# Decoder trunk: rows of x loaded ahead of the modulation weights, and the first channel tile's modulation multiplied by one-column matmuls

## The chip, the core and the metric

One core of a Trainium2 chip runs the whole kernel. TensorE (PE, with its weight loads shown apart as PEld), VectorE (DVE), ScalarE (ACT), GpSimd (POOL) and SyncE (SP) work in parallel, each through its own list of instructions in order. DMAs are issued from the queues of SP, ACT and POOL. Operands lie in SBUF; matmul results lie in PSUM. The metric is the device time of one execution in microseconds (us), lower is better.

## What is computed

A decoder layer over 512 tokens of 1024 channels. What the change touches is its first step, the modulated normalisation and the projection behind it:

```python
cs = jax.nn.silu(c)
...
mod = cs @ w_ada[l] + b_ada[l]
shift1, scale1, gate1, shift2, scale2, gate2 = [m[:, None, :] for m in jnp.split(mod, 6, axis=-1)]
h = _rmsnorm(x, norm1_g[l]) * (1.0 + scale1) + shift1
proj = h @ w_in[l]
```

`_rmsnorm` divides each row of x by the root of its mean square (plus 1e-6) and multiplies by the gain. Behind it stand two attention branches, a gated merge, an output projection and a gated MLP with a short convolution; they are the same before and after.

## The kernel before

The 512 tokens are four row tiles of 128 (`NT`), the 1024 channels eight channel tiles of 128 (`KT`). A large product in float32 is made of three: each operand is split into a rounded high part (type fp32r, a copy) and a low part (the difference), and high x high, low x high and high x low are added in PSUM.

**The first stage** (lines 198 to 413) makes h, transposed to channels x tokens, and the first 768 columns of the projection (six banks `acc6`, one of 128 columns each). It goes by channel tile k. For each, two column blocks of `w_ada` are needed (scale and shift, 8 x 128 rows x 128 columns each, tile `adaw`, two buffers) and one row block of `w_in` (`w0`, 128 x 768, four buffers).

- **Loads** stand on SP's queue in written order (lines 154 and 211 to 226): the conditioning vector c, `adaw` of tile 0, the four row tiles of x (512 KB each), `w0` of tile 0, then `adaw` and `w0` of tile 1, and so on. Bias and gain rows come on ACT's queue (lines 157 to 159).
- **Modulation** of tile k: `ac_ops` multiplies each of the eight row blocks of `adaw` by its entry of silu(c), one value per partition, and sums them, on DVE, 256 columns at a time; `reduce_mod` sums over the partitions by two matmuls with a column of ones; `finish_mod` adds bias and gain, giving one scale and one shift per channel (`mods`).
- **Statistics** of row tile t: `stat` squares on ACT (with the sum) and takes the power -1/2 on POOL (line 174) between DVE steps (lines 170, 180, 184); `normalise` multiplies the first 256 channels on DVE (line 352), `scale_x` the other 768 on ACT (line 375). `turn` transposes channel tile 0 of one row tile on PE (line 357), `h_turn` the later channel tiles.
- **h of tile k**: `h_tile` writes the high part and a full copy on ACT, with scale and shift (line 317); `h_low` makes the low part on DVE (line 321).
- **Weights**: `split_hi` makes the high part of `w0` on ACT (lines 296 and 297, with a reordering of the first 512 columns), `split_lo` the low part on DVE (lines 303 and 305).
- **Products**: `mm_k` runs 6 matmuls for each of three parts (line 327). While tile k multiplies, DVE makes the modulation of tile k + 1.
- `keep_warm(n)` issues n matmuls of ones whose result is not used (line 335), each shown as two PE instructions; 14 stand at the start and 3 behind each row tile.

The order on DVE, ACT and PE is the written one in this stage (`manual_schedule`). In it, before the loop, DVE has the copy of the bias columns `cols`, the modulation of tile 0, and then per row tile t the statistics of t ahead of the normalising of t - 1; the low parts of `w0` of tile 0 come last, directly ahead of the modulation of tile 1 in the loop.

SP's and POOL's queues are ordered by the framework; `va`, a zeroed tile of the attention stage (line 435), is set on POOL early, before the first power.

Of the kernel before, what the change touches and what calls it, by code (L numbers as in the profile page):

```python
# [14 lines left out]
P = 128  # L15
# [11 lines left out]
WB = 3  # L27
# [7 lines left out]
NORM_LAG = 16  # L35
SWA_FILL = (4, 2, 3, 2, 2, 2, 2, 3)
DIFF_FILL = (3, 2, 4, 2)
WARM = 14
GROUPS = ((0,), (1,), (2,), (3,), (4,), (5,), (6,), (7,))
AC_CUT = 7  # L40
MOD_AT = 2
# [11 lines left out]
def kernel(  # L53
# [44 lines left out]
    def tbank(name, shape=(P, S)):  # L98
        return bank("t", 2, list(shape), name)
# [4 lines left out]
    def raw_tile(shape, name):  # L104
        return wp.tile(shape, F32, tag="raw", bufs=4, name=name)
# [45 lines left out]


    crow8 = cpool.tile([8, P], F32, name="crow8")
    nc.sync.dma_start(crow8, c.rearrange("o (a p) -> (o a) p", p=P))
    NR = 16 + 8 + 1
    rows = cpool.tile([NR, P], F32, name="rows")
    nc.scalar.dma_start(rows[0:16, :], b_ada[0, 0 : 2 * D].rearrange("(a p) -> a p", p=P))
# [9 lines left out]
    def rstd_start(ssq, n, d, wpool, plus=None):  # L167
        ms = wpool.tile([P, n], F32, tag="rs_a", bufs=3, name="ms")
        if plus is None:
            nc.vector.tensor_scalar(ms, ssq, 1.0 / d, EPS, ALU.mult, ALU.add)  # L170
        else:
            nc.vector.scalar_tensor_tensor(ms, ssq, 1.0 / d, plus, ALU.mult, ALU.add)  # L172
        r0 = wpool.tile([P, n], F32, tag="rs_c", bufs=3, name="r0")
        nc.gpsimd.tensor_tensor(r0, ms, mhalf[:, :n], ALU.pow)  # L174
        return ms, r0
# [23 lines left out]
    groups = GROUPS  # L199
    adaw, w0 = {}, {}  # L200

    def load_ada(g):
        k, m = g[0], len(g)
        aw = pp.tile([P, 2, KT, m * P], F32, tag="adaw", bufs=2, name=f"adaw{k}")
        for j, base in ((0, D), (1, 0)):
            nc.sync.dma_start(
                aw[:, j], wada[:, base + k * P : base + (k + m) * P].rearrange("(a p) n -> p a n", p=P)
            )
        adaw[k] = aw

    load_ada(groups[0])
    for t in range(NT):
        nc.sync.dma_start(xn[:, t], xd[t * P : (t + 1) * P, :])
    for g in groups:
        if g[0]:
            load_ada(g)
        for k in g:
            r = raw_tile([P, 768], f"w0_{k}")
            nc.sync.dma_start(r, win[k * P : (k + 1) * P, 0:768])
            w0[k] = r  # L220
    nc.sync.dma_start(sink, swa_sinks[0].partition_broadcast(P))
    nc.sync.dma_start(
        lamv.rearrange("p a b -> p (a b)"), diff_lambda[0].rearrange("a b -> (a b)").partition_broadcast(P)
# [8 lines left out]
    nc.vector.tensor_scalar_add(cs, cs, 1.0)  # L232
    nc.vector.reciprocal(cs, cs)
    nc.vector.tensor_mul(cs, cs, pc8)
    pc = tbank("pc", (P, NR))
    nc.tensor.transpose(pc, rows, ident[:NR, :NR])
    cols = cpool.tile([P, NR], F32, name="cols")
    nc.vector.tensor_copy(cols, pc)
    bsh, bsc1, n1g, sublnc = cols[:, 0:8], cols[:, 8:16], cols[:, 16:24], cols[:, 24:25]
    nc.vector.tensor_scalar_add(bsc1, bsc1, 1.0)  # L240
    nc.vector.tensor_scalar_mul(n1g, n1g, -0.5)
    nc.vector.tensor_scalar_mul(sublnc, sublnc, -0.5 * (1.0 - LAM_INIT))
    ac, mods, wts = {}, {}, {}

    def ac_ops(gi, lo, hi):
        g = groups[gi]
        if lo == 0:
            ac[gi] = [pp.tile([P, 2, len(g) * P], F32, tag=f"ac{b}", bufs=2, name=f"ac{gi}_{b}") for b in range(2)]
        aw = adaw[g[0]]
        for kk in range(lo, hi):  # L250
            a = ac[gi][kk % 2]
            if kk < 2:
                nc.vector.tensor_scalar_mul(a, aw[:, :, kk], cs[:, kk : kk + 1])
            else:
                nc.vector.scalar_tensor_tensor(a, aw[:, :, kk], cs[:, kk : kk + 1], a, ALU.mult, ALU.add)
        if hi == KT:
            nc.vector.tensor_add(ac[gi][0], ac[gi][0], ac[gi][1])

    def reduce_mod(gi):
        pas = []  # L260
        for i, k in enumerate(groups[gi]):
            pa = tbank(f"pa{k}", (P, 2))
            for j in range(2):
                nc.tensor.matmul(
                    pa[:, j : j + 1], ac[gi][0][:, j, i * P : (i + 1) * P], ones[:, 0:1], start=True, stop=True
                )
            pas.append(pa)
        return pas

    def finish_mod(gi, pas):  # L270
        for k, pa in zip(groups[gi], pas):
            m = pp.tile([P, 16], F32, tag="mod", bufs=3, name=f"mod{k}")
            nc.vector.scalar_tensor_tensor(
                m[:, 0:1], pa[:, 0:1], bsc1[:, k : k + 1], n1g[:, k : k + 1], ALU.add, ALU.mult
            )
            nc.vector.tensor_add(m[:, 1:2], pa[:, 1:2], bsh[:, k : k + 1])
            mods[k] = m
# [12 lines left out]
    def split_hi(k):  # L290
        pl, nb = (wp, WB) if k % 2 == 0 else (pp, 2)
        wh = pl.tile([P, 768], F32R, tag="whi", bufs=nb, name=f"w0h{k}")
        wl = pl.tile([P, 768], F32R, tag="wlo", bufs=nb, name=f"w0l{k}")
        wts[k] = (wh, wl)
        rq, wq, lq = w0_views(k)
        nc.scalar.copy(wq, rq)
        nc.scalar.copy(wh[:, 512:768], w0[k][:, 512:768])

    def split_lo(k, part):
        wh, wl = wts[k]  # L300
        if part == 0:
            rq, wq, lq = w0_views(k)
            nc.vector.tensor_tensor(lq, rq, wq.bitcast(F32), ALU.subtract)
        else:
            nc.vector.tensor_sub(wl[:, 512:768], w0[k][:, 512:768], wh[:, 512:768].bitcast(F32))
# [8 lines left out]
    def h_tile(k):  # L314
        hf = pp.tile([P, S], F32, tag="hf", bufs=2, name=f"hf{k}")
        for dst in (hTh[k], hf):
            nc.scalar.activation(dst, pts[k], AF.Identity, bias=mods[k][:, 1:2], scale=mods[k][:, 0:1])
        hfs[k] = hf
# [4 lines left out]
    def mm_k(k, part):  # L323
        wh, wl = wts[k]
        lhs, rhs = ((wh, hTh), (wl, hTh), (wh, hTl))[part]
        for i in range(6):
            nc.tensor.matmul(
                acc6[i], lhs[:, i * P : (i + 1) * P], rhs[k],
                start=k == 0 and part == 0, stop=k == KT - 1 and part == 2,
            )  # L330


    def keep_warm(n):
        for i in range(n):
            nc.tensor.matmul(acc6[5][:, :P], ident, ones, start=True, stop=True)

    keep_warm(WARM)
    ac_ops(0, 0, KT)
    rst = pp.tile([P, NT], F32, name="rst")
    half = [None] * NT  # L340

    def stat(t):
        sq = pp.tile([P, D], F32, tag="sq", bufs=1, name=f"sq{t}")
        ss = pp.tile([P, 1], F32, tag="ss", bufs=4, name=f"ss{t}")
        nc.scalar.activation(sq, xn[:, t], AF.Square, accum_out=ss)
        half[t] = rstd_start(ss, 1, D, pp)

    HEAD = 256

    def normalise(t):  # L350
        rstd_end(rst[:, t : t + 1], *half[t], 1, pp)
        nc.vector.tensor_scalar_mul(xn[:, t, :HEAD], xn[:, t, :HEAD], rst[:, t : t + 1])

    pts[0] = tbank("xt0")

    def turn(t):
        nc.tensor.transpose(pts[0][:, t * P : (t + 1) * P], xn[:, t, 0:P], ident)

    for t in range(NT):
        stat(t)  # L360
        if t:
            normalise(t - 1)
            turn(t - 1)
            keep_warm(3)
        if t == 1:
            finish_mod(0, reduce_mod(0))
    split_hi(0)
    normalise(NT - 1)
    turn(NT - 1)
    h_tile(0)  # L370
    split_lo(0, 0)
    split_lo(0, 1)

    def scale_x(t):
        nc.scalar.activation(xn[:, t, HEAD:], xn[:, t, HEAD:], AF.Copy, scale=rst[:, t : t + 1])

    for gi, g in enumerate(groups):
        nxt = groups[gi + 1] if gi + 1 < len(groups) else ()

        for k in nxt:  # L380
            split_hi(k)
        if gi == 0:
            for t in range(NT):
                scale_x(t)

        if nxt:
            ac_ops(gi + 1, 0, AC_CUT)
        h_low(g[0])
        if nxt:
            ac_ops(gi + 1, AC_CUT, KT)  # L390

        for k in g:
            if k == g[0] and len(nxt) == 1:
                h_turn(nxt[0])
            for part in range(3):
                if part == MOD_AT and k == g[-1] and nxt:
                    pas = reduce_mod(gi + 1)
                    split_lo(nxt[0], 0)
                    finish_mod(gi + 1, pas)
                    split_lo(nxt[0], 1)  # L400
                    for n in nxt[1:]:
                        split_lo(n, 0)
                        split_lo(n, 1)
                    for n in nxt:
                        if len(nxt) > 1:
                            h_turn(n)
                        h_tile(n)
                mm_k(k, part)
            if k == g[0]:
                for n in g[1:]:  # L410
                    h_low(n)
# [1313 lines left out]
```

## Time and profile before

| | us |
|---|---|
| median of 3 runs | 722.17 (719.83 to 722.52) |
| the profiled execution | 720.56 |
| its span in the trace | 718.7 |
| first product matmul of tile 0 starts | 18.47 |
| first instruction of tile 1's modulation on DVE | 16.74 |
| last product matmuls of the first stage end | about 59.9 |

Over the span PE is busy 691.1 us (96%), DVE 589.8 (82%), ACT 381.9 (53%) and POOL 84.9 (12%); DMA reads 121.85 MB. A timeline row gives the start, the duration, the engine, the line, the operation with its output and inputs, how many were merged, and in brackets the idle time of the engine before it with what ended it. A merged row's duration runs from the first start to the last end. The stretches table gives the busy time of each engine within a stretch of time, the granted PE clock (1.00 is full) and what the DMA engines moved.

### The profile page before, as it was taken

The numbers are of one execution on the slowest core, as the hardware profiler recorded it, in microseconds if no ns is written. First come the engines' busy times: TensorE is split into PE (matmuls) and PEld (weight loads), VectorE is DVE, ScalarE is ACT, GpSimd is POOL, SyncE is SP. The second block draws the span as 40 slices with busy tenths as digits, with TensorE's granted clock in tenths as the row PEclk, the third lists the DMA queues.
The fourth block names the chain that finished last, engine by engine and source line by source line (L and its number), as shares of the span: only waits on it lengthen the run. The fifth ranks groups of instructions, "written<-read, shape, count | busy, mean of one in ns | idle before, by whom it ended". The sixth has DMA issues, their size and how long they took to land. (4 is left out here: it accounts for less than half of the span.)

```text
span 718.7 us, 11251 instructions
## 1 busy us (share of the span) xinstructions
PE 691.1 (96%) x4172; PEld 603.1 (84%) x4172; DVE 589.8 (82%) x1121; ACT 381.9 (53%) x672; POOL 84.9 (12%) x101
## 2 busy tenths in 40 slices
PE   6998899999999999999999999999999999999994
PEld 6776688777777888888888999999999999778883
DVE  6998877887986674865479899888888999889996
ACT  4643756355553333432358756555656666556662
POOL 4000000000100110000012111111101212640000
PEclk9999999999999999999999999999999999999998
DMA  9986122543543665736717698876879769998502
GB/s 313 305 242 205 60 60 67 169 136 106 169 139 126 206 190 162 235 101 210 246 59 148 162 190 204 207 183 200 201 197 223 161 175 256 206 207 221 178 0 118
DMA packets 117367, 124.70 MB, mean 174 GB/s; under 512 B 4511, under 2 KB 93376, under 8 KB 117312
## 3 DMA queue, kind: packets, MB, share of 16 engines
q1 hardware_dynamic: 98254, 97.71, 43.0%
q0 software_dynamic: 18720, 25.73, 21.0%
q8 instruction: 33, 0.54, 0.3%
q10 hardware_dynamic: 338, 0.54, 0.2%
q14 instruction: 22, 0.18, 0.1%
HBM read 121.85 MB, written 2.11 MB: 172 GB/s over the span
## 5 line engine op out<-in xcount | busy, mean ns | idle before, releaser
L1112 PE MATMUL up<-t,m_whi 128*128 128x256 f32 x528 | 96.1, 283 | 0.0
L1112 PEld LDWEIGHTS up<-t,m_whi 128*128 128x128 f32 x528 | 82.4, 192 | 0.0
L1112 PE MATMUL up<-t,m_wlo 128*128 128x256 f32 x264 | 74.7, 283 | 0.1
L1112 PE MATMUL up<-bh,p_wlo 128*128 128x256 f32 x232 | 65.6, 283 | 0.3 <-DVE p_wlo L1055 0.3
L1112 PE MATMUL up<-bh,p_whi 128*128 128x256 f32 x232 | 65.6, 283 | 0.0
L1112 PE MATMUL up<-bl,p_whi 128*128 128x256 f32 x232 | 65.6, 283 | 0.0
L1112 PEld LDWEIGHTS up<-t,m_wlo 128*128 128x128 f32 x264 | 50.6, 192 | 0.3 <-DVE m_wlo L1055 0.3
L748 DVE SCALAR_TENSOR_TENSOR arow<-ra,cs,arow 128x512 f32<-128x512 f32 x56 | 41.9, 748 | 4.3 <-DMA ra<-in_w_ada_dram 3.6
L1112 PEld LDWEIGHTS up<-bh,p_wlo 128*128 128x128 f32 x232 | 44.5, 192 | 0.5 <-DVE p_wlo L1055 0.5
L1112 PEld LDWEIGHTS up<-bh,p_whi 128*128 128x128 f32 x232 | 44.5, 192 | 0.0
L1112 PEld LDWEIGHTS up<-bl,p_whi 128*128 128x128 f32 x232 | 44.5, 192 | 0.0
L1023 POOL DMA_DIRECT2D s<-in_w_up_dram x21 | 27.3, 1379 | 142.5 <-DMA s<-in_w_up_dram 54.3
L1055 DVE TENSOR_TENSOR m_wlo<-s,m_whi 128x1024 fp32r<-128x1024 f32 x31 | 37.7, 1217 | 2.0 <-ACT m_whi L1051 2.0
L1051 ACT CAST m_whi<-s 128x1024 fp32r<-128x1024 f32 x31 | 32.5, 1047 | 8.5 <-PE up L1112 4.6
L174 POOL TENSOR_TENSOR r<-ms,mhalf 128x1 f32<-128x1 f32 (+1 forms) x16 | 13.6, 848 | 172.4 <-DVE ms L172 105.7
L1112 PE MATMUL up<-t,p_whi 128*128 128x256 f32 x176 | 32.2, 283 | 0.0
L678 ACT ACTIVATE sd<-sd,dmx 128x128 f32<-128x128 f32 (+3 forms) x32 | 17.8, 557 | 22.2 <-DVE dmx L676 15.7
L761 POOL DMA_DIRECT2D mod_rows<-arow x8 | 4.3, 541 | 203.5 <-ACT arow L760 203.4
L1112 PEld LDWEIGHTS up<-t,p_whi 128*128 128x128 f32 x176 | 27.5, 192 | 0.0
L1119 ACT ACTIVATE gT<-a,cv 128x512 f32<-128x512 f32 x22 | 17.7, 814 | 17.6 <-DVE a L1154 17.3
L1051 ACT CAST p_whi<-wa 128x1024 fp32r<-128x1024 f32 x18 | 18.8, 1043 | 12.0 <-PE up L1112 7.2
L1112 PE MATMUL up<-t,p_wlo 128*128 128x256 f32 x88 | 24.9, 283 | 0.0
(476 smaller groups left out, 2120.8 us busy)
## 6 DMA issues: line engine op xcount, KB each, us to landing
ra<-in_w_ada_dram SPq DMA_DIRECT2D x32, 512.0 KB, 4.2
wa<-in_w_up_dram SPq DMA_DIRECT2D x22, 512.0 KB, 4.2
s<-in_w_up_dram SPq DMA_DIRECT2D x21, 512.0 KB, 4.8
s<-in_w_up_dram POOLq DMA_DIRECT2D x21, 512.0 KB, 6.7
adaw<-in_w_ada_dram SPq DMA_DIRECT2D x16, 512.0 KB, 5.0
w<-in_w_in_dram SPq DMA_DIRECT2D x12, 512.0 KB, 4.8
a<-in_w_up_dram SPq DMA_DIRECT2D x11, 512.0 KB, 4.7
b<-in_w_down_dram SPq DMA_DIRECT2D x10, 512.0 KB, 3.6
```

The lines of the kernel that those rows point to most:

```text
L174: nc.gpsimd.tensor_tensor(r0, ms, mhalf[:, :n], ALU.pow)
L678: nc.scalar.activation(pm[m], pm[m], AF.Exp, bias=mx[:, m : m + 1], scale=slope, accum_out=lsum[:, m : m + 1])
L748: nc.vector.scalar_tensor_tensor(ac, r[:, a], cc, ac, ALU.mult, ALU.add)
L761: nc.gpsimd.dma_start(mod_rows[idx : idx + 1, hf * S : (hf + 1) * S], row)
L1023: nc.gpsimd.dma_start(dst, upblock(*blk), accum_op=ALU.add)
L1051: nc.scalar.copy(W[J, name][0], R[J, SRC[name]])
L1055: nc.vector.tensor_sub(lo, R[J, SRC[name]], hi.bitcast(F32))
L1112: nc.tensor.matmul(o[u], w[:, k, cu], b[:, k], start=name in ("p1", "m5", "p2") and k == 0 and x == 0, stop=k == 3 and x == 2, skip_group_ ...
L1119: nc.scalar.activation(grow(j), av[J][:, u], AF.Identity, bias=cv[:, 66 + j : 67 + j], scale=cv[:, 44 + j : 45 + j])
```

## The change

It touches the first stage only.

- c is loaded on ACT's queue. On SP's queue, x rows 0 to 2 come first, then the scale half of tile 0's `adaw` in two pieces, x row 3 in two halves, the shift half in three pieces, `w0` of tile 0 in two pieces, and the rest as before, with tile 1's `adaw` in four pieces.
- Tile 0's modulation leaves DVE. `first_mod` multiplies each 128 x 128 block of `adaw` by the matching column of silu(c) on PE, 16 matmuls with one moving column, summed in PSUM. Scale and shift columns are then finished on DVE as before.
- The written order becomes: statistics, normalising and turn of row tile 0, the columns `cols`, then row tiles 1 to 3 likewise, with the pieces of `first_mod` and two of the four `scale_x` between them. Row tile 3 is squared in two halves. The initial `keep_warm` is 8 in place of 14, and the later ones are two of 2 in place of three of 3.
- For tile 0, the high part of the first 512 columns of `w0` is made on DVE in place of ACT, and the high and low parts come after the modulation is finished. `mm_k(0, ...)` takes its six column groups in the order 4, 5, 0, 1, 2, 3.

```diff
-WARM = 14
+WARM = 8
...
-    nc.sync.dma_start(crow8, c.rearrange("o (a p) -> (o a) p", p=P))
+    nc.scalar.dma_start(crow8, c.rearrange("o (a p) -> (o a) p", p=P))
...
-    load_ada(groups[0])
-    for t in range(NT):
-        nc.sync.dma_start(xn[:, t], xd[t * P : (t + 1) * P, :])
...
+    adaw[0] = pp.tile([P, 2, KT, P], F32, tag="adaw", bufs=2, name="adaw0")
+    for t in range(NT - 1):
+        load_x(t)
+    load_first(0, (0, 4, 8))
+    load_x(NT - 1, (0, S, D))
+    load_first(1, (0, 4, 6, 8))
+    load_w0(0, (512, 768))
+    load_w0(0, (0, 512))
+    for g in groups[1:]:
+        load_ada(g, (0, 4, 8) if g[0] == 1 else (0, 8))
+        load_w0(g[0])
...
-        for i in range(6):
+        for i in (4, 5, 0, 1, 2, 3) if k == 0 else range(6):
...
-    keep_warm(WARM)
-    ac_ops(0, 0, KT)
...
+        for lo, hi in ((0, D),) if t < NT - 1 else ((0, S), (S, D)):
+            sq = pp.tile([P, D], F32, tag="sq", bufs=1, name=f"sq{t}_{lo}")
+            ss = pp.tile([P, 1], F32, tag="ss", bufs=5, name=f"ss{t}_{lo}")
+            nc.scalar.activation(sq[:, lo:hi], xn[:, t, lo:hi], AF.Square, accum_out=ss)
+            if hi < D:
+                nc.vector.tensor_scalar(ss, ss, 1.0 / D, EPS, ALU.mult, ALU.add)
+                plus = ss
+        half[t] = rstd_start(ss, 1, D, pp, plus)
...
+    keep_warm(WARM)
+    stat(0)
+    normalise(0)
...
+    turn(0)
+    keep_warm(2)
+    pc = tbank("pc", (P, NR))
+    nc.tensor.transpose(pc, rows, ident[:NR, :NR])
+    cols = cpool.tile([P, NR], F32, name="cols")
+    nc.vector.tensor_copy(cols, pc)
...
+    pa0 = tbank("pa0", (P, 2))
+    stat(1)
+    normalise(1)
+    turn(1)
+    keep_warm(2)
+    stat(2)
+
+    def first_mod(j, lo, hi):
+        for kk in range(lo, hi):
+            nc.tensor.matmul(
+                pa0[:, j : j + 1], adaw[0][:, j, kk], cs[:, kk : kk + 1], start=kk == 0, stop=kk == KT - 1
+            )
+
+    first_mod(0, 0, 4)
+    scale_x(0)
+    normalise(2)
+    first_mod(0, 4, 8)
+    turn(2)
+    stat(3)
+    scale_x(1)
+    first_mod(1, 0, 4)
+    m0 = mods[0] = pp.tile([P, 16], F32, tag="mod", bufs=3, name="mod0")
+    nc.vector.scalar_tensor_tensor(m0[:, 0:1], pa0[:, 0:1], bsc1[:, 0:1], n1g[:, 0:1], ALU.add, ALU.mult)
+    normalise(3)
+    first_mod(1, 4, 6)
+    turn(3)
+    first_mod(1, 6, 8)
+    nc.vector.tensor_add(m0[:, 1:2], pa0[:, 1:2], bsh[:, 0:1])
...
+    nc.scalar.copy(wts[0][0][:, 512:768], w0[0][:, 512:768])
+    rq, wq, lq = w0_views(0)
+    nc.vector.tensor_copy(wq, rq)
+    split_lo(0, 1)
     h_tile(0)
+    scale_x(2)
+    scale_x(3)
     split_lo(0, 0)
-    split_lo(0, 1)
```

More of the change, by code (lines that the diff above doesn't have):

```diff
@@ L200, with load_ada, load_x, load_first @@
     adaw, w0 = {}, {}
-    def load_ada(g):
+    def load_ada(g, cuts=(0, KT), whole=()):
         k, m = g[0], len(g)
[L204 to L209, printed above, removed]
-    load_ada(groups[0])
-    for t in range(NT):
-        nc.sync.dma_start(xn[:, t], xd[t * P : (t + 1) * P, :])
[L214 to L220, printed above, removed]
+        aw = adaw[k] = pp.tile([P, 2, KT, m * P], F32, tag="adaw", bufs=2, name=f"adaw{k}")
+        for lo, hi in zip(cuts, cuts[1:]):
+            for j, base in ((0, D), (1, 0)):
+                src = wada[lo * P : hi * P, base + k * P : base + (k + m) * P].rearrange("(a p) n -> p a n", p=P)
+                nc.sync.dma_start(aw[:, j, lo:hi], src)
+    def load_x(t, cols=(0, D)):
+        for lo, hi in zip(cols, cols[1:]):
+            nc.sync.dma_start(xn[:, t, lo:hi], xd[t * P : (t + 1) * P, lo:hi])
+    def load_first(j, cuts):
+        base = (D, 0)[j]
+        for lo, hi in zip(cuts, cuts[1:]):
+            src = wada[lo * P : hi * P, base : base + P].rearrange("(a p) n -> p a n", p=P)
+            nc.sync.dma_start(adaw[0][:, j, lo:hi], src)
+    def load_w0(k, cuts=(0, 768)):
+        if k not in w0:
+            w0[k] = raw_tile([P, 768], f"w0_{k}")
+        for lo, hi in zip(cuts, cuts[1:]):
+            nc.sync.dma_start(w0[k][:, lo:hi], win[k * P : (k + 1) * P, lo:hi])
+    adaw[0] = pp.tile([P, 2, KT, P], F32, tag="adaw", bufs=2, name="adaw0")
[9 more added lines that the diff above has]
+        load_w0(g[0])
     nc.sync.dma_start(sink, swa_sinks[0].partition_broadcast(P))
@@ L234 @@
     nc.vector.tensor_mul(cs, cs, pc8)
[L235 to L242, printed above, removed]
     ac, mods, wts = {}, {}, {}
@@ L342, in stat, with scale_x @@
     def stat(t):
[L343 to L346, printed above, removed]
+        plus = None
+        for lo, hi in ((0, D),) if t < NT - 1 else ((0, S), (S, D)):
[6 more added lines that the diff above has]
+        half[t] = rstd_start(ss, 1, D, pp, plus)
     HEAD = 256
+    def scale_x(t):
+        nc.scalar.activation(xn[:, t, HEAD:], xn[:, t, HEAD:], AF.Copy, scale=rst[:, t : t + 1])
     def normalise(t):
@@ L357, in turn @@
         nc.tensor.transpose(pts[0][:, t * P : (t + 1) * P], xn[:, t, 0:P], ident)
[L359 to L369, printed above, removed]
+    turn(0)
[4 more added lines that the diff above has]
+    nc.vector.tensor_copy(cols, pc)
+    bsh, bsc1, n1g, sublnc = cols[:, 0:8], cols[:, 8:16], cols[:, 16:24], cols[:, 24:25]
+    nc.vector.tensor_scalar_add(bsc1, bsc1, 1.0)
+    nc.vector.tensor_scalar_mul(n1g, n1g, -0.5)
+    nc.vector.tensor_scalar_mul(sublnc, sublnc, -0.5 * (1.0 - LAM_INIT))
+    pa0 = tbank("pa0", (P, 2))
[24 more added lines that the diff above has]
+    nc.vector.tensor_add(m0[:, 1:2], pa0[:, 1:2], bsh[:, 0:1])
+    wts[0] = tuple(wp.tile([P, 768], F32R, tag=f"w{b}", bufs=WB, name=f"w0{b}0") for b in ("hi", "lo"))
+    nc.scalar.copy(wts[0][0][:, 512:768], w0[0][:, 512:768])
+    rq, wq, lq = w0_views(0)
+    nc.vector.tensor_copy(wq, rq)
+    split_lo(0, 1)
     h_tile(0)
+    scale_x(2)
+    scale_x(3)
     split_lo(0, 0)
-    split_lo(0, 1)
-    def scale_x(t):
-        nc.scalar.activation(xn[:, t, HEAD:], xn[:, t, HEAD:], AF.Copy, scale=rst[:, t : t + 1])
     for gi, g in enumerate(groups):
@@ L381 @@
             split_hi(k)
-        if gi == 0:
-            for t in range(NT):
-                scale_x(t)
         if nxt:
```

## The prediction

> **What bounds the kernel now.** I read the busy table by stretches of time first, then the timeline of the first 40 us, then the clock column in half-microsecond stretches. The loop over the eight channel tiles runs until about 60 us:
>
> ```profile
> 30.00:35.00 5.00, 4.90 (x26) 3.88 (x25) 4.81 (x15) 1.92 (x5) 0.00 (x0) 1.00 0.88 264
> ```
>
> The columns are PE, PEld, DVE, ACT, POOL, clock, DMA share and GB/s. DVE is busy 4.81 of 5.00 us and PE 4.90, ACT 1.92, and DMA moves 264 GB/s. Which of DVE and PE sets the pace shows in the first instruction of each tile's modulation on DVE:
>
> ```profile
> 16.74 0.61 DVE L253 TENSOR_SCALAR ac<-adaw,cs 128x256 f32<-128x256 f32 x2
> ...
> 22.42 0.61 DVE L253 TENSOR_SCALAR ac<-adaw,cs 128x256 f32<-128x256 f32 x2
> ...
> 27.90 0.61 DVE L253 TENSOR_SCALAR ac<-adaw,cs 128x256 f32<-128x256 f32 x2
> ...
> 33.24 0.61 DVE L253 TENSOR_SCALAR ac<-adaw,cs 128x256 f32<-128x256 f32 x2
> ...
> 37.40 0.52 PEld L264 LDWEIGHTS pa<-ones,ac 128*128 128x128 f32 x4 [0.46 <-issue]
> ...
> 38.58 0.61 DVE L253 TENSOR_SCALAR ac<-adaw,cs 128x256 f32<-128x256 f32 x2
> ```
>
> The period settles at 38.58 - 33.24 = 5.34 us, and PE stands 0.46 us ahead of its reduction, which I read as the wait for the DVE sum that it reduces. So DVE paces this stage, and what counts is **when DVE begins tile 1's modulation, 16.74 now**. The first two periods (5.68 and 5.48) hold 0.48 us of DVE waiting beyond 5.34. After the loop, work follows from work, and I find nothing tied to absolute time; a shift goes to the end one for one.
>
> **What precedes 16.74.**
>
> ```profile
> 1.19 1.03 SPq L206 DMA_DIRECT2D adaw<-in_w_ada_dram  x2
> ...
> 4.72 1.80 POOL L435 MEMSET va<- 128x2048 f32 x1
> ...
> 7.11 2.46 DVE L255 SCALAR_TENSOR_TENSOR ac<-adaw,cs,ac 128x256 f32<-128x256 f32 x6
> 8.32 1.06 ACT L345 ACTIVATE sq<-xn 128x1024 f32<-128x1024 f32 x1 [5.35 <-DMA xn<-in_x_dram]
> 9.29 0.19 ACT L345 ACTIVATION_READ_ACCUMULATOR sq<-xn 128x1 f32 x1
> ...
> 11.29 0.35 DVE L352 TENSOR_SCALAR xn<-xn,rst 128x256 f32<-128x256 f32 x1
> 11.70 0.14 PEld L357 LDWEIGHTS xt<-ident,xn 128*128 128x128 f32 x1 [0.68 <-DVE xn L352]
> ...
> 11.87 0.83 PE L335 MATMUL a<-ones,ident 128*128 128x128 f32 x6
> ...
> 12.54 0.50 PE L264 MATMUL pa<-ones,ac 128*128 128x1 f32 x4
> 13.08 0.22 DVE L273 SCALAR_TENSOR_TENSOR mod<-pa,cols 128x1 f32<-128x1 f32 x1 [1.44 <-PE pa L264]
> ...
> 13.22 0.15 DVE L276 TENSOR_TENSOR mod<-pa,cols 128x1 f32<-128x1 f32 x1
> ```
>
> Tile 0's modulation, which the change takes off DVE, was under way at 7.11, while the first x rows landed only at 8.32: DVE had nothing else to do then. DVE keeps the written order: the 1.44 us before 13.08 is DVE standing for a PE result that was queued behind a transpose and warming matmuls. That kind of wait decides the new order.
>
> **The change, part by part.**
>
> *Loads.* From the first adaw issue to x0's landing is 8.32 - 1.19 = 7.13 us, for 1.05 MB of adaw and 0.52 MB of x.
>
> ```profile
> 3.50:4.00 0.50, 0.00 (x0) 0.00 (x0) 0.38 (x3) 0.00 (x0) 0.50 (x2) 1.00 1.13 342
> ...
> 7.50:8.00 0.50, 0.50 (x5) 0.50 (x4) 0.50 (x3) 0.00 (x0) 0.00 (x0) 1.00 1.00 401
> ```
>
> At 342 and 401 GB/s that is 3.07 + 1.31 us of moving and 2.75 us of delay. With the conditioning vector on ACT's queue, x0 can be issued at about 0.74, where SP starts now (an estimate: 1.19 less one issue), and lands at 0.74 + 2.75 + 1.31 = 4.8; x1 at 6.1, x2 7.4, the scale half 9.0, x3 10.3, the shift half 11.8, w0 12.8, tile 1's weights 15.8. The gain at the source is real: 3.5 us for x0.
>
> *The row chain.* The squares of x0 end at 4.8 + 1.16 = 6.0, but the power runs on POOL, whose memset of va ends at 6.52 (same place in POOL's queue, as nothing ahead of it changes). From there on the pace is that of one tile's statistics:
>
> ```profile
> 13.79 0.35 DVE L352 TENSOR_SCALAR xn<-xn,rst 128x256 f32<-128x256 f32 x1
> 14.06 0.15 DVE L170 TENSOR_SCALAR ms<-ss 128x1 f32<-128x1 f32 x1
> ...
> 14.35 0.70 POOL L174 TENSOR_TENSOR r<-ms,mhalf 128x1 f32<-128x1 f32 x1 [0.18 <-DVE ms L170]
> ...
> 15.08 0.22 DVE L180 SCALAR_TENSOR_TENSOR rt<-r,ms 128x1 f32<-128x1 f32 x1
> 15.34 0.16 DVE L184 SCALAR_TENSOR_TENSOR rst<-rt,r 128x1 f32<-128x1 f32 x1
> ...
> 15.53 0.35 DVE L352 TENSOR_SCALAR xn<-xn,rst 128x256 f32<-128x256 f32 x1
> ```
>
> From ms to xn is 15.53 - 14.06 = 1.47 us, and the next ms follows xn by 14.06 - 13.79 = 0.27. Before, ms of tile t+1 was written ahead of the normalising of tile t, so that POOL's time was covered; now the order is stat, normalise, stat, normalise, and each tile pays 1.74. Tile 0: power 6.55, xn 7.73 to 8.08, transpose 8.14.
>
> *The columns.* DVE's next instruction is the copy of cols, which waits for a PE transpose placed behind the turn and two warming matmuls (four instructions).
>
> ```profile
> 4.86 0.27 PE L236 MATMUL pc<-ident,rows 25*128 25x25 f32 x1 [2.10 <-DMA rows<-in_diff_subln_g_dram]
> 5.05 6.16 PE L335 MATMUL a<-ones,ident 128*128 128x128 f32 x28
> 5.16 0.19 DVE L238 COPY cols<-pc 128x25 f32<-128x25 f32 x1 [1.21 <-PE pc L236]
> 5.38 1.17 DVE L240 TENSOR_SCALAR cols<-cols 128x8 f32<-128x8 f32 x1
> 5.46 1.10 DVE L241 TENSOR_SCALAR cols<-cols 128x8 f32<-128x8 f32 x1
> ...
> 14.20 0.41 PE L357 MATMUL xt<-ident,xn 128*128 128x128 f32 x1 [1.15 <-DVE ms L170]
> ...
> 14.40 1.50 PE L335 MATMUL a<-ones,ident 128*128 128x128 f32 x6
> ...
> 15.69 0.42 PE L357 MATMUL xt<-ident,xn 128*128 128x128 f32 x1
> ```
>
> Seven PE instructions took 15.69 - 14.20, 0.213 us each, at the low clock; six took 12.54 - 11.87, 0.112 each, at the high one. The 28 at the start fit the low one (27 x 0.213 + 0.42 = 6.17), so PE starts cold although the clock column, which has no entry yet, prints 1.00. Hence pc at 8.14 + 5 x 0.213 = 9.21, the copy at 9.51, and four short issues (0.22 and 0.08 each) later ms1 at 9.97. Squares of x1 have been ready since 7.3, so this wait is new and costs some 2.2 us of the head start. Then xn1 11.44 to 11.79, turn 11.85; xn2 13.18; ms3 (with its extra half-row step) 13.6, power 13.9 to 14.6.
>
> *Modulation on PE.* Sixteen one-column matmuls are 32 PE instructions, since two are x4 in the row at 12.54: 0.125 us each there. The trace has none at the low clock; the bounds are 0.125 and 0.213, and I take 0.213, because loading 128x128 weights is the bulk of both kinds. The clock:
>
> ```profile
> 14.00:14.50 0.50, 0.30 (x2) 0.30 (x3) 0.46 (x4) 0.09 (x1) 0.32 (x2) 0.81 1.15 348
> ...
> 17.50:18.00 0.50, 0.50 (x5) 0.42 (x3) 0.50 (x2) 0.36 (x1) 0.00 (x0) 0.78 1.15 344
> ```
>
> It falls to half at 14.31 (0.38 of the first stretch at half) and returns at 17.72, 3.5 us after PE became steadily busy at 14.20; at the start it took about 6 us, from 4.86 to the end of the 28. In the new order PE has holes until the turn at 11.85, so release comes between 15.4 and 17.9; I take 17.7. The Trainium skill, "TensorE: Matmul & The Clock Gate", Part 1, says that the gate judges activity in free-running windows of about 3.4 us; the spacing 17.72 - 14.31 = 3.41 agrees, and by that rule alone release could come at any point from 15.3 to 18.7, that is +2.7 to +4.1 instead of one value.
>
> PE from 11.85: turn and four warming instructions to 12.92; scale half, 16 x 0.213, to 16.33. DVE's m0 scale stands ahead of normalise(3): 16.37, then xn3 16.96 to 17.31, 2.4 us later than the power allowed. PE: turn(2) to 16.54, twelve of the shift half (5.5 slow, 6.5 fast) to 18.52, turn(3) 18.65, the last four 19.15. m0 shift at 19.19. DVE then does the copy that ACT did, and both low parts.
>
> ```profile
> 15.80 0.68 DVE L303 TENSOR_TENSOR w0l<-w,w0h 128x512 fp32r<-128x512 f32 x1
> ...
> 16.40 0.42 DVE L305 TENSOR_TENSOR w0l<-w,w0h 128x256 fp32r<-128x256 f32 x1
> ```
>
> They issue 0.60 and 0.34 apart; the 512-wide copy I price as the 512-wide subtraction, 0.60 (from 0.35, the 256-wide xn, to 0.68). 19.33 + 0.60 + 0.34 + 0.60 = 20.87 for tile 1's modulation: 4.13 late. The 0.48 us of early DVE waits goes away, as PE is done by then. **Sum: +3.65 us.** At 0.125 throughout, m0 shift comes at 16.70, DVE at 18.38: +1.16. At 0.213 throughout, 20.20 and 21.88: +4.66. Scaling x on ACT and the six channel groups' order cost nothing: ACT is idle 3 us of each 5.
>
> **Rivals.** (1) *Not slower: data sets the pace.* If DVE met no wait (power overlapped, columns and modulation done in PE's holes), xn3 would follow x3: landing 10.3, half-row square 0.8, chain 1.8, DVE 12.9, tile 1 at 14.5, its weights landing in halves from 14.3. That is 2.2 + 0.48 = 2.7 us faster. For it: the loads do arrive so. Against: the 1.44 us wait shows that order binds; it decides from where m0 shift is ready before 13. (2) *Matmuls of one column count as idle* and PE stays cold into tile 0's product: +4.66, and twelve product matmuls at twice their 3.2 us end 1.4 us after the DVE sum: up to +6. (3) *PE releases early or short ones aren't slowed:* +1.2 to +2.6. (4) *Tile 2's weights come late:* their slot is now freed by PE at 19.15, not by DVE at 9.57, and SP's later loads queue behind.
>
> ```profile
> DMA to landing us min/median/max: 3.7/5.0/9.5
> ```
>
> With 0.5 us for the second issue they land at 24.7, against 20.87 + 5.34 = 26.2; at 9.5 us it is +3 more, +6.6 in all. (5) *The shift is absorbed later:* 0.
>
> **How the numbers follow.** The profiled execution took 720.56 us (span 718.7); the three runs' median is 722.17. The mean of the four is 721.3, and I add to it: 725.0, own range 723.9 (release at 15.4) to 726.0 (no release by then). Chances: forecast 0.45; (2) and (4) together 0.18, at 726 to 728; (3) 0.17, at 722.5 to 723.9; (5) 0.05, 721.3; (1) 0.15, 718.6. The range 721 to 728 leaves out (1) and little else. About 0.5% (3.6 us) is what can be told from no change: three quarters of the forecast, with the spread of the runs, and all of (2) and (4) are slower, 0.52; of (1) half reaches faster, 0.08; the rest is 0.40.
>
> **What would show it.** Right: DVE idle before the cols copy and before both m0 steps with PE as releaser, ms instructions 1.7 us apart, half clock while the one-column matmuls run, tile 1's first DVE instruction near 21, periods of 5.34 behind it. Wrong: that instruction before 17, or DMA as the releaser of xn and m0, or a pitch of 0.125 at the low clock.

## The result, and the profile after

| | before | after |
|---|---|---|
| median of 5 runs, us | 721.78 (719.83 to 722.52) | 725.76 (724.65 to 726.66) |
| ratio to before, 95% interval | | 1.0059 (1.0044 to 1.0074) |
| the profiled execution, us | 720.56 | 725.57 |
| tile 1's modulation begins on DVE, us | 16.74 | 21.64 |
| ACT takes up the first stage's last bank, us | 58.82 | 63.50 |

The kernel became 0.6% slower, 3.98 us by the medians; the forecast was 725.0. The timeline of DVE in the kernel after, from the copy of the columns to tile 3's modulation:

```profile
9.52 0.18 DVE L382 COPY cols<-pc 128x25 f32<-128x25 f32 x1 [1.66 <-PE pc L380]
...
9.96 0.14 DVE L170 TENSOR_SCALAR ms<-ss 128x1 f32<-128x1 f32 x1
...
11.49 0.15 DVE L170 TENSOR_SCALAR ms<-ss 128x1 f32<-128x1 f32 x1
...
18.01 0.22 DVE L409 SCALAR_TENSOR_TENSOR mod<-pa,cols 128x1 f32<-128x1 f32 x1 [4.58 <-PE pa L396]
...
18.59 0.35 DVE L367 TENSOR_SCALAR xn<-xn,rst 128x256 f32<-128x256 f32 x1
20.30 0.16 DVE L414 TENSOR_TENSOR mod<-pa,cols 128x1 f32<-128x1 f32 x1 [1.36 <-PE pa L396]
20.37 0.42 DVE L418 CAST w0hi<-w 128x512 fp32r<-128x512 f32 x1
20.71 0.42 DVE L314 TENSOR_TENSOR w0lo<-w,w0hi 128x256 fp32r<-128x256 f32 x1
...
21.64 0.61 DVE L262 TENSOR_SCALAR ac<-adaw,cs 128x256 f32<-128x256 f32 x2
...
27.22 0.61 DVE L262 TENSOR_SCALAR ac<-adaw,cs 128x256 f32<-128x256 f32 x2
...
32.56 0.61 DVE L262 TENSOR_SCALAR ac<-adaw,cs 128x256 f32<-128x256 f32 x2
```

DVE stands three times for PE: 1.66 us for the transposed columns, 4.58 for the scale column, 1.36 for the shift column. Behind that, the loop runs as before, one period of 5.58 us and then 32.56 - 27.22 = 5.34. What PE did meanwhile, in its timeline of the kernel after:

```profile
11.63 0.48 PE L375 MATMUL xt<-ident,xn 128*128 128x128 f32 x1 [2.14 <-DVE ms L170]
...
12.75 3.41 PE L396 MATMUL pa<-cs,adaw 128*128 128x1 f32 x16
...
16.27 1.71 PE L396 MATMUL pa<-cs,adaw 128*128 128x1 f32 x8
18.29 1.01 PE L396 MATMUL pa<-cs,adaw 128*128 128x1 f32 x4 [0.31 <-DVE mod L409]
...
19.41 0.85 PE L396 MATMUL pa<-cs,adaw 128*128 128x1 f32 x4
...
21.32 2.93 PE L336 MATMUL a<-hThA,w0hi 128*128 128x512 f32 x6
24.05 2.26 PE L336 MATMUL a<-hThA,w0lo 128*128 128x512 f32 x6
...
28.34 1.64 PE L336 MATMUL a<-hThA,w0h 128*128 128x512 f32 x6
```

Sixteen PE instructions of one column took 3.41 us, 0.213 each: as long as the 128-column ones at the low clock in the kernel before. And the first six product matmuls of tile 0 take 2.93 us, the next six 2.26, where six take 1.64 later: **the clock was still low when the product began**. Counted by durations, about three of the second six are slow, so it rose near 25.4.

The loads did arrive early. The squares of the first rows on ACT, in the kernel after, began 3.93 us sooner than the 8.32 of before:

```profile
4.39 1.06 ACT L354 ACTIVATE sq<-xn 128x1024 f32<-128x1024 f32 x1 [0.77 <-DMA xn<-in_x_dram]
...
63.50 2.42 ACT L472 ACTIVATE qa<-a,qsc 128x512 fp32r<-128x512 f32 x4 [1.84 <-PE a L336]
...
75.83 1.05 ACT L114 CAST w_h<-w 128x1024 fp32r<-128x1024 f32 x1 [3.45 <-PE pq L119]
```

The last two of these rows and the same two of the kernel before show the shift at the end of the first stage, and one step into the second:

```profile
58.82 2.43 ACT L427 ACTIVATE qa<-a,qsc 128x512 fp32r<-128x512 f32 x4 [1.83 <-PE a L327]
...
71.67 1.05 ACT L114 CAST w_h<-w 128x1024 fp32r<-128x1024 f32 x1 [3.44 <-PE pq L119]
```

+4.68 at the stage's end, +4.16 at the next. Later, from the chain of waits (start, us, what), before and then after:

```profile
383.60 14.31 PE up L1112 x120
...
602.85 7.47 DMA t<-in_w_down_dram
...
633.84 59.24 PE dc L1669 x260
```

```profile
387.07 14.31 PE up L1157 x120
...
606.32 8.56 DMA t<-in_w_down_dram
...
638.85 59.26 PE dc L1714 x260
```

+3.47 at the MLP's start, and +5.01 behind its transfers: two that stand in the chain took 8.56 and 11.05 us in this execution instead of 7.47 and 10.60, and they are the same code. So the profiled pair overstates the difference (5.01 us of time) against the medians (3.98); the shift that the first stage hands on is 3.5 to 4.2 us.

### The profile page after: what moved, and what is told of

The parts are those of the page before. It is cut to its first block, busy times and chain, and to the rows that moved or that the text cites. A ratio compares the mean times of both kernels' runs of the same rounds, so it can differ in the third digit from the quotient of the medians.

```text
span 723.8 us, 11262 instructions
## 1 busy us (share of the span) xinstructions
PE 695.9 (96%) x4178; PEld 607.0 (84%) x4178; DVE 585.4 (81%) x1114; ACT 381.3 (53%) x673; POOL 84.5 (12%) x101
## 5 line engine op out<-in xcount | busy, mean ns | idle before, releaser
L1164 ACT ACTIVATE gT<-a,cv 128x512 f32<-128x512 f32 x22 | 17.7, 812 | 17.6 <-DVE a L1199 17.3
```

The lines of the kernel that those rows point to most:

```text
L1164: nc.scalar.activation(grow(j), av[J][:, u], AF.Identity, bias=cv[:, 66 + j : 67 + j], scale=cv[:, 44 + j : 45 + j])
```

## The experiments

Each kernel is the kernel after with one part changed, unless said otherwise. Ratios are to the kernel before, run beside it on the same chip (its median 720.33 us in the runs with the first four, 721.79 with the next four, 721.23 with the last). Beside the total I read two places: the start of tile 1's modulation on DVE (before 16.74, after 21.64) and ACT's start on the last bank (58.82, 63.50).

| | tile 1 begins | last bank | ratio, 95% |
|---|---|---|---|
| e1, columns earlier | 20.18 | 62.28 | 1.0061 (1.0035 to 1.0087) |
| e2, PE kept busy ahead of the one-column matmuls | 18.69 | 60.34 | 1.0017 (0.9995 to 1.0040) |
| e3, modulation of tile 0 on DVE again | 18.82 | 61.47 | 1.0037 (1.0021 to 1.0053) |
| e4, modulation weights ahead of x again | 25.62 | 67.24 | 1.0114 (1.0085 to 1.0144) |
| e5, scale and shift in two PSUM tiles | 21.16 | 62.78 | one run, 727.11 us |
| e6, statistics one row tile ahead | 21.04 | 62.66 | one run, 725.75 us |
| e7, an order of its own | 15.66 | 58.20 | 1.0019 (1.0001 to 1.0038) |
| e8, before with one-column warming | 18.01 | 61.23 | one run, 721.18 us |
| e9, scale half on DVE, shift half on PE | 16.87 | 60.36 | 0.9985 (0.9969 to 1.0001) |

### e1: the columns transposed and copied ahead of the first normalising

```diff
-    keep_warm(WARM)
+    keep_warm(WARM - 2)
+    pc = tbank("pc", (P, NR))
+    nc.tensor.transpose(pc, rows, ident[:NR, :NR])
+    keep_warm(2)
     stat(0)
+    cols = cpool.tile([P, NR], F32, name="cols")
+    nc.vector.tensor_copy(cols, pc)
...
     normalise(0)
...
     turn(0)
     keep_warm(2)
-    pc = tbank("pc", (P, NR))
-    nc.tensor.transpose(pc, rows, ident[:NR, :NR])
-    cols = cpool.tile([P, NR], F32, name="cols")
-    nc.vector.tensor_copy(cols, pc)
...
```

> The bias columns are transposed behind six of the eight first warming matmuls and copied on DVE ahead of the first normalising; nothing else is moved. Theory (DVE and PE stand for each other in the written order, and PE multiplies the first modulation at the low clock): DVE no longer stands 1.7 us before the copy, the second row tile's mean square starts near 7.8 us in place of 9.96, the first one-column matmul near 10.5 in place of 12.75, and DVE begins tile 1's modulation near 19.5 in place of 21.64; the time falls by about 2.1 us to 723.7. Rival (the landing of the shift half and of w0 sets the end of the first modulation): tile 1 still begins at about 21.6 and the time stays at 725.8.

The timeline of PE in e1 shows why the gain is smaller: the bias rows came late, and PE stood for them.

```profile
7.04 0.27 PE L371 MATMUL pc<-ident,rows 25*128 25x25 f32 x1 [0.72 <-DMA rows<-in_diff_subln_g_dram]
```

The copy followed at 7.35, in the middle of row tile 0's statistics instead of after its normalising. Tile 1 begins at 20.18, 1.46 us earlier than after; its first period is longer (5.82 us instead of 5.58), so that the cast at 75.83 comes at 74.59, 1.24 earlier. In the total it can't be told apart from the kernel after: one suspect of several, and not the largest.

### e2: eight more warming matmuls behind the column transpose

```diff
-WARM = 8
+WARM = 10
...
     nc.tensor.transpose(pc, rows, ident[:NR, :NR])
+    keep_warm(8)
     cols = cpool.tile([P, NR], F32, name="cols")
```

> Two more warming matmuls at the start and eight behind the transposition of the bias columns, in PE's hole, so that PE works without a hole of over 0.5 us from 3.3 us on. Theory: the clock is full by 10.2 at the latest, one-column matmuls then take 0.125 us for each PE instruction in place of 0.213, and tile 1's modulation begins between 18.4 (clock full until the last of them) and 20 (clock falls on the way, if one-column matmuls don't count as work); the time falls by 1.6 to 3.2 us. Rival (their pitch comes from loading the weights and not from the clock): the pitch stays at 0.213, tile 1 begins at 21.6 or a little later, and the time doesn't fall.

The timeline of PE in e2:

```profile
9.44 2.99 PE L344 MATMUL a<-ones,ident 128*128 128x128 f32 x16
...
12.82 1.84 PE L397 MATMUL pa<-cs,adaw 128*128 128x1 f32 x16
...
18.37 2.92 PE L336 MATMUL a<-hThA,w0hi 128*128 128x512 f32 x6 [0.15 <-ACT hThA L326]
```

Sixteen one-column instructions now take 1.84 us, 0.115 each, instead of 3.41. Tile 1 begins 2.95 us earlier, with nothing changed but the warming matmuls, and the total no longer differs from before by more than the interval. This is the largest single part: **most of the loss was the low clock under the one-column matmuls**. But the product is cold again at 18.37: PE had been busy from 9.44 almost without a hole, and the clock fell at 18.26, 0.95 us behind the last one-column matmul.

### e3: tile 0's modulation on DVE, all else as after

```diff
-    first_mod(0, 0, 4)
     scale_x(0)
...
-    first_mod(1, 0, 4)
-    m0 = mods[0] = pp.tile([P, 16], F32, tag="mod", bufs=3, name="mod0")
...
+    ac_ops(0, 0, KT)
+    pas = reduce_mod(0)
     normalise(3)
...
     turn(3)
-    first_mod(1, 6, 8)
-    nc.vector.tensor_add(m0[:, 1:2], pa0[:, 1:2], bsh[:, 0:1])
+    finish_mod(0, pas)
```

> The loads and the written order of the changed kernel, but tile 0's modulation goes back to DVE (eight products and a sum, then two reductions on PE), between the last mean square and the last normalising. Theory: DVE has nothing to do there but wait, so its 3.5 us run from 13.5 to 17.0, both columns are finished near 18.0, and tile 1's modulation begins near 19.4; the time falls by about 2.2 us to 723.6, still above before's 721.8 because the rows remain in series. Rival (the modulation on PE costs nothing, what was lost lies in the loads or in the rows' order alone): taking it off PE adds DVE's 3.5 us, tile 1 begins after 21.6 and the time rises.

The timeline of e3, one row of PE and then DVE:

```profile
8.12 0.61 PE L344 MATMUL a<-ones,ident 128*128 128x128 f32 x4
...
12.80 0.61 DVE L262 TENSOR_SCALAR ac<-adaw,cs 128x256 f32<-128x256 f32 x2
...
15.82 0.42 DVE L266 TENSOR_TENSOR ac<-ac,ac 128x256 f32<-128x256 f32 x1
...
17.35 0.22 DVE L282 SCALAR_TENSOR_TENSOR mod<-pa,cols 128x1 f32<-128x1 f32 x1 [0.39 <-PE pa L273]
...
18.82 0.61 DVE L262 TENSOR_SCALAR ac<-adaw,cs 128x256 f32<-128x256 f32 x2
```

DVE makes all of it from 12.80 to 16.16, in the time in which it stood for PE in the kernel after, and tile 1 begins 2.82 us earlier. Not all of that is the modulation's: in this execution the clock was up behind the first row tile (the row at 8.12 takes 0.61 us, the same four instructions 1.06 in the kernel after), the columns were copied at 8.93 instead of 9.52, and the rows behind them came 0.59 us sooner. That leaves 2.2 us. So moving this work off DVE gained nothing here: DVE was free, and PE at the low clock took longer (7.5 us, from 12.75 to 20.26).

### e4: the modulation weights of tile 0 ahead of x again

```diff
+    load_first(0, (0, 4, 8))
+    load_first(1, (0, 4, 6, 8))
     for t in range(NT - 1):
         load_x(t)
-    load_first(0, (0, 4, 8))
     load_x(NT - 1, (0, S, D))
-    load_first(1, (0, 4, 6, 8))
```

> The changed kernel with tile 0's modulation weights loaded ahead of the rows of x again, in the same pieces. Theory: the loads ahead did bring their gain and the new order spent it; with the rows 3.5 us later again, the whole chain moves back: tile 1's modulation begins near 25.2 in place of 21.64 and the time rises by about 3.6 us to 729.4. Rival (the loads' order does nothing in this stage): tile 1 still begins near 21.6 and the time stays at 725.8.

The timeline of DVE in e4:

```profile
10.21 0.15 DVE L170 TENSOR_SCALAR ms<-ss 128x1 f32<-128x1 f32 x1 [5.92 <-ACT sq L354]
...
25.62 0.61 DVE L262 TENSOR_SCALAR ac<-adaw,cs 128x256 f32<-128x256 f32 x2
```

Tile 1 begins 25.62 - 21.64 = 3.98 us later. The first half of the change does what it says and is worth 4 us in this order; the second half spends it and 4.9 more. What the early loads are worth in the old order was not run.

### e5: the shift column in a PSUM tile of its own

```diff
-    pa0 = tbank("pa0", (P, 2))
+    pas0 = [tbank("pa0", (P, 2))[:, 0:1], acc6[0][:, 0:1]]
...
-                pa0[:, j : j + 1], adaw[0][:, j, kk], cs[:, kk : kk + 1], start=kk == 0, stop=kk == KT - 1
+                pas0[j], adaw[0][:, j, kk], cs[:, kk : kk + 1], start=kk == 0, stop=kk == KT - 1
...
```

> The changed kernel with the shift column summed in another PSUM bank than the scale column. Theory: DVE's step on the scale column waited until 18.01, although its eight matmuls ended at 16.2, because both columns are one tile; with two banks it runs near 16.2 and the last row tile is normalised by 17.2 in place of 18.9; but PE, at the low clock and without a hole, ends the shift half only 0.3 us earlier (its own stand behind that step goes), so tile 1's modulation begins near 21.3 in place of 21.64. Rival (DVE's 4.58 us wait is itself the loss): tile 1 begins 1.7 us earlier, near 19.9.

The timeline of DVE in e5:

```profile
16.19 0.22 DVE L409 SCALAR_TENSOR_TENSOR mod<-pa,cols 128x1 f32<-128x1 f32 x1 [2.77 <-PE pa L396]
...
21.16 0.61 DVE L262 TENSOR_SCALAR ac<-adaw,cs 128x256 f32<-128x256 f32 x2
```

The scale step comes at 16.19 instead of 18.01: it had waited for the first four matmuls of the shift half too, as long as both columns lay in one tile. PE's 0.31 us of waiting for that step, in the row at 18.29 above, is gone with it. It brings 0.48 us at tile 1, since the shift half still ends late. The new tile lies in another bank too; which of the two counts was not tried.

### e6: the statistics of row tile t + 1 ahead of the normalising of t

```diff
     stat(0)
+    stat(1)
     normalise(0)
...
-    stat(1)
+    stat(2)
     normalise(1)
     turn(1)
     keep_warm(2)
-    stat(2)
...
     scale_x(0)
+    stat(3)
     normalise(2)
...
     turn(2)
-    stat(3)
     scale_x(1)
```

> The changed kernel with the mean square of row tile t + 1 written ahead of the normalising of t on DVE, as it was before the change. Theory: the power of the second row tile is ready before the bias columns are copied, so its transpose comes near 10.8 in place of 11.63 and the one-column matmuls, back to back at the low clock behind it, all come 0.8 us earlier: tile 1's modulation begins near 20.8. Rival (the series of rows is the loss, 3 x 0.7 us of POOL's power): it begins near 19.5.

The timeline of DVE in e6:

```profile
21.04 0.61 DVE L262 TENSOR_SCALAR ac<-adaw,cs 128x256 f32<-128x256 f32 x2
```

0.60 us earlier than after: the power on POOL is covered again, but what comes behind still waits for PE.

### e7: columns late, statistics ahead, one-column matmuls in the holes of PE

```diff
+    pas0 = [acc6[0][:, 0:1], acc6[1][:, 0:1]]
...
     turn(0)
-    keep_warm(2)
     pc = tbank("pc", (P, NR))
     nc.tensor.transpose(pc, rows, ident[:NR, :NR])
+    keep_warm(3)
+    stat(1)
+    stat(2)
+    normalise(1)
+    turn(1)
+    scale_x(0)
+    first_mod(0, 0, 4)
+    keep_warm(1)
+    normalise(2)
+    turn(2)
+    first_mod(0, 4, 8)
+    keep_warm(1)
     cols = cpool.tile([P, NR], F32, name="cols")
     nc.vector.tensor_copy(cols, pc)
...
     stat(3)
     scale_x(1)
...
+    normalise(3)
     first_mod(1, 0, 4)
...
     turn(3)
...
+    keep_warm(1)
+    first_mod(1, 4, 8)
...
     split_lo(0, 1)
+    split_lo(0, 0)
+    nc.vector.tensor_add(m0[:, 1:2], pas0[1], bsh[:, 0:1])
     h_tile(0)
```

with 10 instead of 8 matmuls in the first `keep_warm`.

> The loads and the one-column matmuls of the changed kernel in another written order: bias columns copied where DVE waits for the last row tile, mean squares of rows 1 and 2 ahead of the normalising of row 1, warming matmuls in PE's early holes, the two columns summed in two banks, and the high and low parts of tile 0's weights ahead of the shift column. Theory: the rows are ready near 12.5, the one-column matmuls run at the full clock in part and end between 14 and 15.5, and tile 1's modulation begins between 14.4 and 16.5, ahead of before's 16.74; the time is 0.5 to 2.7 us below before's. Rival (the landing of tile 1's weights or PE's low clock in tile 0's product eats it): tile 1 begins before 16.5, but the periods behind it are over 5.34 and the time is not below before's.

The timeline of DVE in e7:

```profile
15.66 0.61 DVE L262 TENSOR_SCALAR ac<-adaw,cs 128x256 f32<-128x256 f32 x2
...
21.39 0.22 DVE L282 SCALAR_TENSOR_TENSOR mod<-pa,cols 128x1 f32<-128x1 f32 x1 [1.08 <-PE pa L273]
...
21.93 0.61 DVE L262 TENSOR_SCALAR ac<-adaw,cs 128x256 f32<-128x256 f32 x2
```

Tile 1 begins 1.08 us ahead of the kernel before, but its first period is 6.27 us: the product of tile 0 is cold, and DVE waits 1.08 us behind it for PE's reduction. The last bank is 0.62 ahead. The rest goes at the start of the second stage, in the stretches of e7 (PE, PEld, DVE, ACT, POOL, clock, DMA share, GB/s):

```profile
67.50:68.00 0.50, 0.50 (x3) 0.41 (x2) 0.50 (x4) 0.00 (x0) 0.00 (x0) 0.50 0.87 258
```

and in the timeline of PE, first of e7 and then of the kernel before:

```profile
69.17 1.65 PE L125 MATMUL sw<-ka,qa 64*128 64x256 f32 x12
```

```profile
69.25 0.97 PE L125 MATMUL sw<-ka,qa 64*128 64x256 f32 x12
```

The clock fell to half there, and the same twelve matmuls took 1.65 us instead of 0.97; ACT's next cast comes at 72.26, 0.59 behind the 71.67 of the kernel before. The total is 1.0019, just above no change.

### e8: the kernel before, its first 14 warming matmuls cut to one column

```diff
-    keep_warm(WARM)
+    for i in range(WARM):
+        nc.tensor.matmul(acc6[5][:, :1], ident, ones[:, 0:1], start=True, stop=True)
```

> The kernel before the change, in which only the 14 first warming matmuls multiply one column in place of 128 (their results aren't used). Theory (one-column matmuls don't count as work for the clock gate): they still take about 0.213 us for each PE instruction, but the clock isn't released by 11.7 as it was before: the six warming instructions behind the first row tile take 1.3 us in place of 0.67. Rival (PE being occupied is enough): those six take 0.67 us as before.

This is the disputed point by itself. The timeline of PE in e8:

```profile
5.03 6.13 PE L338 MATMUL a<-ones,ident 128*128 128x1 f32 x28
...
12.19 1.49 PE L335 MATMUL a<-ones,ident 128*128 128x128 f32 x6
```

The 28 instructions take 6.13 us, where the 128-column ones took 6.16; PE looks equally busy. Yet the six warming instructions behind the first row tile take 1.49 us instead of 0.83: the clock was not released. One execution could miss a release by where it falls: the changes in the clock column stand about 3.41 us or a multiple of it apart (14.31 and 17.72 in the kernel before), and 6.13 us is less than twice that. e4 settles it. Its clock is at half from 10.57 to 27.64, five times 3.41, and the third of these five is, in the stretches of e4:

```profile
17.40:20.81 3.41, 3.41 (x18) 3.41 (x18) 0.01 (x1) 0.00 (x0) 0.55 (x1) 0.50 0.23 93
```

PE was occupied in all of it, by one transpose and otherwise by one-column matmuls, and the clock stayed at half. **One-column matmuls cost the same time and didn't count as work for the clock.** Where the time went in e8 is another matter. DVE in e8, near the end of the stage:

```profile
54.31 1.22 DVE L115 TENSOR_TENSOR w_l<-w,w_h 128x1024 fp32r<-128x1024 f32 x1
55.45 0.41 DVE L257 TENSOR_TENSOR ac<-ac,ac 128x256 f32<-128x256 f32 x1
```

and ACT in e8, one step into the second:

```profile
71.65 1.05 ACT L114 CAST w_h<-w 128x1024 fp32r<-128x1024 f32 x1 [3.43 <-PE pq L119]
```

The last bank was 2.41 us late, and the next step came at 71.65, as before (71.67). A low part for the second stage (54.31) stands ahead of the last modulation's sum here (in the kernel before it comes behind, at 54.82), so I take the lateness to be partly work done in advance, in time that DVE spent waiting in the kernel before. The stage's end alone is no measure where the order behind it moves; e3 and e9 have the same order as e8 at this place.

### e9: e7 with the scale half on DVE and more warming

```diff
     turn(1)
+    keep_warm(5)
     scale_x(0)
-    first_mod(0, 0, 4)
-    keep_warm(1)
+    scale_ops(0, 4)
     normalise(2)
     turn(2)
-    first_mod(0, 4, 8)
-    keep_warm(1)
+    keep_warm(2)
+    stat(3)
+    scale_ops(4, 8)
+    first_mod(1, 0, 4)
+    nc.tensor.matmul(pas0[0], acs[0], ones[:, 0:1], start=True, stop=True)
+    scale_x(1)
+    normalise(3)
+    first_mod(1, 4, 8)
+    turn(3)
     cols = cpool.tile([P, NR], F32, name="cols")
...
+    nc.vector.tensor_add(m0[:, 1:2], pas0[1], bsh[:, 0:1])
     split_lo(0, 1)
     split_lo(0, 0)
-    nc.vector.tensor_add(m0[:, 1:2], pas0[1], bsh[:, 0:1])
```

This diff is against e7. `scale_ops` is the sum of `ac_ops` over the 128 columns of the scale half alone.

> As the reordered kernel, but the scale half of tile 0's modulation goes back to DVE (eight products of 128 columns and a sum, placed where DVE waits for the last row tile), only the shift half stays in one-column matmuls, and the hole that this leaves on PE before them is filled with seven warming matmuls. Theory: PE works on 128 columns until the shift half lands, so the clock stays full through the shift half and tile 0's product; the shift column is finished near 14, tile 1's modulation begins near 15.2 and tile 2's near 20.6 (the reordered kernel: 15.66 and 21.93, with 1.08 us of waiting for PE); the first stage ends near 57 in place of before's 58.8 and the time is 0.5 to 2 us below before's. Rival (what is gained in the first stage is given back where the second begins, in DVE's wait for the streamed rows of the later modulation): the stage ends near 57, but the time is within 0.5 us of before's.

The timeline of DVE in e9:

```profile
16.87 0.61 DVE L262 TENSOR_SCALAR ac<-adaw,cs 128x256 f32<-128x256 f32 x2
...
28.34 0.62 DVE L262 TENSOR_SCALAR ac<-adaw,cs 128x256 f32<-128x256 f32 x2 [0.48 <-DMA adaw<-in_w_ada_dram]
```

Tile 1 begins as late as before, and later than expected; the clock was at half from 10.28 to 13.69 and again from 17.11 to 20.52, so the product was cold once more (its first six matmuls took 2.80 us), and tile 3's weights were late once. The last bank comes at 60.36 where 57 was expected, yet ACT's next cast comes at 70.70, 0.97 us ahead of the kernel before. The total of 0.9985 is the best of all, but its interval reaches 1.0001: 12 runs don't tell it apart from the kernel before, and no version here clearly beats it.

## Why the prediction held, and where it did not

**Right.** The forecast was +3.65 us with tile 1 at 20.87; measured were +3.98 and 21.64. The mechanism was as described: rows land early, the new written order and PE's low clock spend more than that. That the two sums lie so close is partly luck, as what follows shows.

- *Rows.* x0 was put at 4.8 and was in use at 4.39. e4 prices the early loads at 4.0 us; the prediction had 3.5 at the source.
- *Columns.* The copy was put at 9.51 and came at 9.52; the second ms at 9.97, and came at 9.96. The wait was priced at 2.2 us of the head start, where the prediction's own rows give 9.97 - 8.00 = 1.97 (ms follows the xn at 7.73 by 0.27); e1 recovers 1.46.
- *Row period.* 1.74 us was forecast, 11.49 - 9.96 = 1.53 measured: POOL's power took 0.55, less than the 0.70 that I used. The first one-column matmul, put at 12.92, started at 12.75.
- *Pitch.* 0.213 us at the low clock, from between 0.125 and 0.213, was right, and e2 shows 0.115 at the high one.

**The step that failed** is the release of the clock, put at 17.7 within 15.4 to 17.9. It came near 25.4, as the first half of rival (2) has it: one-column matmuls count as idle (e8, e4). The all-low case of the prediction gave 20.20 for the shift step and 21.88 for tile 1; measured were 20.30 and 21.64. The second half of that rival, a further loss at tile 0's product up to +6, was too large: the cold product cost DVE a first period of 5.58 instead of 5.34, 0.24 us, so that of the 0.48 us that I wanted back, half came. The Trainium skill, "TensorE: Matmul & The Clock Gate", Part 1, says that the gate watches a free-running activity window of about 3.4 us and doesn't count instructions. Read with busy as the timeline shows it, that rule has the clock released within two windows of PE's work from 11.63 to 20.26, where the one hole is 0.31 us; it wasn't, nor in e4's window without a hole, and the measurement decides: how busy PE looks in the timeline isn't what the gate sees.

**Two smaller steps missed, and partly cancelled.**

- *The scale step* was put at 16.37 and came at 18.01. I had read the two columns as independent; in one PSUM tile they are not, for the reader on DVE or for PE behind it (e5). It cost 0.48 us at tile 1. (The 2.4 us that the prediction has xn3 behind the power is 1.9 by its own rows: xn follows the power's end by 0.48.)
- *The 512-wide copy* was priced at 0.60 from a subtraction; the next instruction issued 20.71 - 20.37 = 0.34 behind it. That gave back 0.26.

With the shift step 1.11 us late, the copy 0.26 short and the rest 0.08 short, 20.87 becomes 21.64. Tile 1 was thus 0.77 worse than forecast, which with the missing half of the recoup makes +4.66 at the last tile (the last bank shows +4.68). "Work follows from work, a shift goes to the end one for one" was nearly right: 0.5 us was absorbed at the first boundary. The first stage's end came 1.0 us later than forecast, and this absorption took half of it back, so the total looks better than its terms were.

**Rivals.** Tile 2's weights late, (4): no, no wait stands at 27.22. Absorbed later, (5): 0.5 us of 4.7. Data setting the pace, (1): e7 shows how near that was, tile 1 at 15.66 with the same loads, and yet no gain in the total.

**What the parts are worth** at tile 1, each alone: the clock under the one-column matmuls 2.95 us (e2), the modulation back on DVE 2.82 (e3, with 0.59 of it from the clock behind the first row tile), the columns 1.46 (e1), the statistics in series 0.60 (e6), the shared PSUM tile 0.48 (e5). They aren't to be added, since each shortens a stretch that the others end in as well.

**Open.** The trace tells which matmuls were slow, not what the gate measures: whether it is columns streamed or something else was not tried beyond one column against 128. Each of these profiles is one execution, so the exact time of a release is not known to better than one such.

## What to carry to other kernels

Before moving work from one engine to another, look whether the first was waiting anyway and at which clock the second runs: here DVE was free, and PE at half clock took 7.5 us for what DVE did in 3.4. Loads brought forward by 4 us help only as far as the written order lets the early data be used, so move the waits on an in-order engine together with the loads. Keep TensorE warm with matmuls that have many columns, and give results that are read at different times PSUM tiles of their own.

## What the runs showed that I had not expected

- 28 PE instructions of one column took 6.13 us, against 6.16 for 128 columns, and left the clock at half (e8). A clock that was up fell again within a microsecond behind 4.5 us of them (e2).
- The clock fell to half at the start of the second stage (in e7 from about 67.4 to 70.8) in the profiles of e4, e5, e6 and e7 and not in the other seven. It cost about 1.5 us: ACT stands 4.88 to 4.95 us before its cast in these four and 3.27 to 3.45 in the others. Edits that differ only in the first stage moved when such a fall comes. The other executions have no trace, but each has a mean granted clock: 0.985 to 0.991 in the twelve of e7, against 0.990 to 0.997 in the kernel before beside it, and e7's three at 0.991 took 721.0 to 721.6 us. So most executions of e7 had more of the low clock; at which place was seen in one.
- DVE's next instruction issued 0.34 us behind a rounding copy of 512 columns from SBUF, as soon as behind a subtraction of 256 columns (20.37 to 20.71, 20.71 to 21.04).
